# Row-wise infinity norm: the loads change queues after the 24th, GpSimd's setup waits for row 0, output copies are issued last

## The chip, the cores and the metric

One core of a Trainium2 chip runs the kernel. The metric is the device time of one execution in microseconds, as the median of several runs. Smaller is better.

## The reference

```
x: float32 [8192, 8192], normally distributed
out = np.linalg.norm(x, ord=np.inf, axis=1)      # out[i] = max over j of |x[i, j]|, float32 [8192]
```

The whole input, 268 MB, has to be read once. The output is 32 KB.

## The kernel before, in words

The 8192 rows are 64 groups of 128, one row of a group on each of the 128 partitions. The code calls such a group a "row" (R = 64). VectorE does all the arithmetic: `absmax` (line 62) is one tensor_reduce with the operation max and the absolute value, which takes a stretch of a row in SBUF to one number per partition. A dense reading of the loop (lines 90 to 138) goes like this.

- **Units.** The list PIECES (lines 18 to 24) has 36 units. Units 0 to 3 (HEAD) are single rows of 8192 elements. Units 4 to 26 are pairs: two rows of x that are neighbours in memory lie behind one another on the same partition, so one load brings 16384 elements (64 KB) per partition, 4096 KB for each row of the pair. Units 27 to 31 are pairs cut into two or three pieces, and units 32 to 35 are single rows cut into ever smaller pieces, the last of 896 elements.
- **The ring.** Loads land in `ring`, which holds three pairs (RING = 3 * 16384 elements per partition). Buffers are taken one after the other; `at` goes back to zero at the end. A load into a part of the ring waits for the data that landed there before, and for the VectorE instruction that read them. The very last piece has a tile of its own, `last`.
- **The loads.** Line 108 issues all 53 of them on SyncE (SP), in the order of the program.
- **The partial maxima.** Rows 0 to 47 go straight to `res` (63 columns, lines 118 to 121). Rows from CUT = 48 up, the four single rows of HEAD among them (rows 56 to 59), come in up to K = 4 pieces, each to a column of its own in `part` (line 130). The pieces of the very last row go into the last columns of `last` (line 128), so that its final reduction (line 110) takes them along.
- **Setup.** GpSimd clears `part` (line 52, since not every row has four pieces) and makes the identity matrix `ident` (line 54: a memset and an affine_select), which TensorE uses to transpose.
- **The output.** After the unit before the last, line 134 takes `part` to the last 15 columns of `res`. `pairs_out` (lines 77 to 86) transposes 56 columns on TensorE, ScalarE copies the result from PSUM and stores it by its own queue; `singles_out` (lines 67 to 75) does the same for 7 columns. The last row is transposed at line 142, copied by VectorE and stored by SP (lines 143 and 144).

The tile framework puts in the semaphore waits; each engine and each queue works through its instructions in order.

Of the kernel before, what the change touches and what calls it, by code (L numbers as in the profile page):

```python
# [1 line left out]

# [5 lines left out]

P = 128
FP32 = mybir.dt.float32  # L10
MAX = mybir.AluOpType.max

HEAD = 4
PAIRS = 28
PIECES = (
    [[8192]] * HEAD
    + [[16384]] * 23  # L20
    + [[8192, 8192], [7232, 9152], [6720, 9664], [8640, 7744], [5568, 5568, 5248]]
    + [[4480, 3712], [3392, 1920, 2880], [2752, 1600, 2048, 1792]]
    + [[1792, 1664, 1472, 1280, 1088, 896]]
)
RING = 3 * 16384


CUT = 48
K = 4


@with_exitstack
def kernel(
    ctx: ExitStack,
    tc: tile.TileContext,
    x: bass.AP,
    out: bass.AP,
):
    nc = tc.nc
    n_rows, n_cols = x.shape  # L40
    R = n_rows // P
    assert R == 64 and n_cols == 8192

    X_ONE = 2 * PAIRS

    single = ctx.enter_context(tc.tile_pool(name="single", bufs=1))
    psum_pool = ctx.enter_context(tc.tile_pool(name="psum", bufs=1, space=bass.MemoryType.PSUM))

    ring = single.tile([P, RING], FP32)
    res = single.tile([P, R - 1], FP32)  # L50
    part = single.tile([P, R - 1 - CUT, K], FP32)
    nc.gpsimd.memset(part, 0.0)  # L52
    ident = single.tile([P, P], FP32)
    make_identity(nc, ident)


    n_last = len(PIECES[-1]) - 1
    w_last = PIECES[-1][-1]
    last = single.tile([P, w_last + n_last], FP32)
    fin = single.tile([P, 1], FP32)  # L60

    def absmax(dst, src):
        nc.vector.tensor_reduce(  # L63
            out=dst, in_=src, axis=mybir.AxisListType.X, op=MAX, apply_absolute_value=True,
        )

    def singles_out():
        n = R - 1 - X_ONE
        ps = psum_pool.tile([n, P], FP32, name="ps_singles")
        sb = single.tile([n, P], FP32, name="sb_singles")  # L70
        nc.tensor.transpose(ps, res[:, X_ONE:], ident)  # L71
        nc.scalar.copy(sb, ps)  # L72
        nc.scalar.dma_start(
            out=out[X_ONE * P : (R - 1) * P].rearrange("(r p) -> r p", p=P), in_=sb
        )

    def pairs_out():
        sb = single.tile([PAIRS, P, 2], FP32, name="sb_pairs")
        both = res[:, :X_ONE].rearrange("p (g r) -> p g r", r=2)
        for r in range(2):  # L80
            ps = psum_pool.tile([PAIRS, P], FP32, name=f"ps_pairs{r}")
            nc.tensor.transpose(ps, both[:, :, r], ident)  # L82
            nc.scalar.copy(sb[:, :, r], ps)  # L83
        nc.scalar.dma_start(
            out=out[: X_ONE * P].rearrange("(g p r) -> g p r", p=P, r=2), in_=sb
        )

    at = 0
    next_pair, next_one = 0, X_ONE
    for u, widths in enumerate(PIECES):  # L90
        k = sum(widths) // n_cols
        if k == 2:
            row, next_pair = next_pair, next_pair + 2
        else:
            row, next_one = next_one, next_one + 1
        src = x[row * P : (row + k) * P].rearrange("(p r) m -> p (r m)", r=k)
        off = 0
        n_part = {}
        for h, w in enumerate(widths):
            final = u == len(PIECES) - 1 and h == n_last  # L100
            if final:
                buf = last[:, :w]
            else:
                if at + w > RING:
                    at = 0
                buf = ring[:, at : at + w]
                at += w
            nc.sync.dma_start(out=buf, in_=src[:, off : off + w])  # L108
            if final:
                absmax(fin[:, :1], last)  # L110
                break
            s = 0
            while s < w:
                r = row + (off + s) // n_cols
                left = n_cols - (off + s) % n_cols
                c = (w - s) // n_cols if left == n_cols else 0
                if c and r + c <= CUT:
                    absmax(
                        res[:, r : r + c],
                        buf[:, s : s + c * n_cols].rearrange("p (c m) -> p c m", m=n_cols),  # L120
                    )
                    s += c * n_cols
                    continue
                e = min(w, s + left)
                i = n_part.get(r, 0)
                n_part[r] = i + 1
                if r == R - 1:
                    absmax(last[:, w_last + i : w_last + i + 1], buf[:, s:e])
                else:
                    absmax(part[:, r - CUT, i : i + 1], buf[:, s:e])  # L130
                s = e
            off += w
        if u == len(PIECES) - 2:
            nc.vector.tensor_reduce(  # L134
                out=res[:, CUT:], in_=part, axis=mybir.AxisListType.X, op=MAX,
            )
            pairs_out()
            singles_out()

    fin_ps = psum_pool.tile([1, P], FP32)  # L140
    fin_sb = single.tile([1, P], FP32)
    nc.tensor.transpose(fin_ps, fin, ident)  # L142
    nc.vector.tensor_copy(out=fin_sb, in_=fin_ps)  # L143
    nc.sync.dma_start(out=out[(R - 1) * P :].rearrange("(r p) -> r p", p=P), in_=fin_sb)


# [1 line left out]
_INS = ['x']  # L148
_OUTS = [((8192,), 'float32')]


# [23 lines left out]
```

## Time and profile before

| what | us |
|---|---|
| median of 3 runs (630.62 to 630.86) | 630.73 |
| the profiled execution | 630.84 |
| its span, from the first to the last instruction | 629.1 |
| VectorE busy, 59 instructions | 552.6 (88% of the span) |
| one reduction of a pair, 16384 elements | 17.22 |
| one reduction of a row, 8192 elements | 8.69 |
| median from issue to landing of a pair's load | 40.8 |
| issue of the last load, line 108 | 614.48 |
| reduction of `part`, line 134 | 617.12 |
| last store issued, line 144 | 627.13 |

The DMA engines moved 268.49 MB at a mean of 427 GB/s over the span. All loads are on the queue q1 (SP's, 7634 packets), the two early stores on q10 (ScalarE's, 56 packets). ScalarE's other work is 2.0 us in all, GpSimd's 0.8 us and TensorE's 1.2 us.

How to read it: the views of waits give the engine, the instruction, what it waited for, then the total, the number of times and the longest. The timeline gives start, duration, engine, line and operation, and in brackets the idle time before it with what ended it. The table by stretches gives the stretch and its length, then the busy time of TensorE, its weight loads, VectorE, ScalarE and GpSimd, the clock of TensorE, the DMA engines' share and GB/s. DMA lines give the queue, its packets, MB and the share of 16 engines' time.

### The profile page before, as it was taken

Reading aid. Unit: us, or ns where it says so; the run is one execution under the profiler, and the core shown is the slowest. Engines: PE = TensorE matmul, PEld = TensorE weight load, DVE = VectorE, ACT = ScalarE, POOL = GpSimd, SP = SyncE. Lnnn points to the kernel's source line nnn. Section 1 sums busy time; section 2 is a strip of 40 time slices with the busy share of each in tenths; the row PEclk is TensorE's granted clock in tenths of the full one; section 3 lists DMA queues with packets and bytes.
Section 4 is the critical chain, followed back from the end, with each engine's and each line's share of the span. In section 5 each row is a group of like instructions: output and inputs, shape, how many; then the busy total and the mean of one; then the engine's idle time right before and its main releaser. Section 6 shows DMA issues by size and latency. Waiting matters only on the chain.

```text
span 629.1 us, 217 instructions
## 1 busy us (share of the span) xinstructions
PE 1.2 (0%) x4; PEld 0.3 (0%) x4; DVE 552.6 (88%) x59; ACT 2.0 (0%) x4; POOL 0.8 (0%) x7
## 2 busy tenths in 40 slices
PE   0000000000000000000000000000000000000000
PEld 0000000000000000000000000000000000000000
DVE  1983988889988889888898888998888999999998
ACT  0000000000000000000000000000000000000000
POOL 0000000000000000000000000000000000000000
DMA  8999999999999999999999999999999999999996
GB/s 367 433 467 404 463 404 463 400 467 404 463 404 463 404 463 404 463 404 463 404 463 404 463 408 458 408 458 408 458 408 429 431 447 432 427 426 424 425 423 265
DMA packets 7692, 268.49 MB, mean 427 GB/s; under 512 B 870, under 2 KB 906, under 8 KB 2058
## 3 DMA queue, kind: packets, MB, share of 16 engines
q1 hardware_dynamic: 7634, 268.44, 99.0%
q10 hardware_dynamic: 56, 0.03, 0.0%
q14 instruction: 2, 0.02, 0.0%
HBM read 268.44 MB, written 0.03 MB: 427 GB/s over the span
## 4 chain that ended last, share of the span: by engine, by line
DMA 57%; DVE 43%; issue 0%; SPq 0%; PE 0%
DMA ring<-in_x_dram 57%; DVE res L63 25%; DVE part L63 17%; DVE last L63 1%; DVE fin L63 0%; SPq L108 0%; PE fin_ps L142 0%; DVE fin_sb L143 0%; DVE res L134 0%
## 5 line engine op out<-in xcount | busy, mean ns | idle before, releaser
L63 DVE TENSOR_REDUCE res<-ring 128x2 f32<-128x16384 f32 (+1 forms) x25 | 413.2, 16536 | 57.6 <-DMA ring<-in_x_dram 57.6
L63 DVE TENSOR_REDUCE part<-ring 128x1 f32<-128x8192 f32 (+19 forms) x26 | 130.0, 5067 | 16.3 <-DMA ring<-in_x_dram 16.3
L63 DVE TENSOR_REDUCE last<-ring 128x1 f32<-128x1792 f32 (+4 forms) x5 | 8.0, 1662 | 0.0
L83 ACT COPY sb_pairs<-ps_pairs 28x128 f32<-28x128 f32 x2 | 0.5, 264 | 615.9 <-PE ps_pairs L82 615.9
L82 PE MATMUL ps_pairs<-ident,res 128*28 128x128 f32 x2 | 0.6, 394 | 617.5 <-DVE res L134 617.5
L83 ACT ACT_TABLE_LOAD x1 | 1.3, 1283 | 0.7 <-PEq L159 0.7
L63 DVE TENSOR_REDUCE fin<-last 128x1 f32<-128x901 f32 x1 | 1.1, 1091 | 0.0
L143 DVE COPY fin_sb<-fin_ps 1x128 f32<-1x128 f32 x1 | 0.3, 279 | 0.5 <-PE fin_ps L142 0.5
L82 PEld LDWEIGHTS ps_pairs<-ident,res 128*28 128x28 f32 x2 | 0.1, 106 | 617.5 <-issue 617.5
L71 PE MATMUL ps_singles<-ident,res 128*7 128x128 f32 x1 | 0.4, 417 | 0.0
L142 PE MATMUL fin_ps<-ident,fin 128*1 128x128 f32 x1 | 0.4, 373 | 8.1 <-DVE fin L63 8.1
masks.py:199 POOL TENSOR_SCALAR_AFFINE_SELECT ident<-ident 128x128 f32<-128x128 f32 x1 | 0.3, 292 | 0.1
L72 ACT COPY sb_singles<-ps_singles 7x128 f32<-7x128 f32 x1 | 0.3, 254 | 0.0
L134 DVE TENSOR_REDUCE res<-part 128x15 f32<-128x60 f32 x1 | 0.2, 216 | 0.0
masks.py:197 POOL MEMSET ident<- 128x128 f32 x1 | 0.2, 204 | 0.0
L52 POOL MEMSET part<- 128x60 f32 x1 | 0.1, 148 | 0.3 <-POOLq L159 0.3
L71 PEld LDWEIGHTS ps_singles<-ident,res 128*7 128x7 f32 x1 | 0.1, 132 | 0.1
L159 POOL MEMSET const-bfloat16-1.0<- 128x1 bf16 x1 | 0.1, 102 | 0.0
L159 POOL MEMSET const-uint8-127<- 128x1 uint8 x1 | 0.1, 102 | 0.0
L159 POOL MEMSET const-float32-0.0<- 128x1 f32 x1 | 0.1, 98 | 0.2 <-issue 0.2
L159 POOL MEMSET const-float32-1.0<- 128x1 f32 x1 | 0.1, 98 | 0.0
L142 PEld LDWEIGHTS fin_ps<-ident,fin 128*1 128x1 f32 x1 | 0.1, 80 | 8.6 <-DVE fin L63 8.6
## 6 DMA issues: line engine op xcount, KB each, us to landing
ring<-in_x_dram SPq DMA_DIRECT2D x6, 4096.0 KB, 21.7
ring<-in_x_dram SPq DMA_DIRECT2D x2, 2784.0 KB, 39.3
ring<-in_x_dram SPq DMA_DIRECT2D x1, 4832.0 KB, 40.7
ring<-in_x_dram SPq DMA_DIRECT2D x1, 4576.0 KB, 40.6
ring<-in_x_dram SPq DMA_DIRECT2D x1, 4320.0 KB, 34.1
ring<-in_x_dram SPq DMA_DIRECT2D x1, 3872.0 KB
ring<-in_x_dram SPq DMA_DIRECT2D x1, 3616.0 KB, 30.1
ring<-in_x_dram SPq DMA_DIRECT2D x1, 3360.0 KB
```

The costliest lines, as they stand in the source:

```text
L52: nc.gpsimd.memset(part, 0.0)
L63: nc.vector.tensor_reduce(out=dst, in_=src, axis=mybir.AxisListType.X, op=MAX, apply_absolute_value=True,)
L71: nc.tensor.transpose(ps, res[:, X_ONE:], ident)
L72: nc.scalar.copy(sb, ps)
L82: nc.tensor.transpose(ps, both[:, :, r], ident)
L83: nc.scalar.copy(sb[:, :, r], ps)
L134: nc.vector.tensor_reduce(out=res[:, CUT:], in_=part, axis=mybir.AxisListType.X, op=MAX,)
L142: nc.tensor.transpose(fin_ps, fin, ident)
L143: nc.vector.tensor_copy(out=fin_sb, in_=fin_ps)
L159: nc = _bacc.Bacc("TRN2", target_bir_lowering=False, num_devices=1)
```

## The change

Four things are different.

1. The first HEAD + SP_PAIRS = 24 units are loaded by SP as before, and all later ones by ScalarE's queue. The call `keep_in_program_order` keeps the issue order as written.
2. GpSimd's setup stands in a function `setup`, called once, after the first row's reduction. Both memsets get a manual dependency on that reduction. The memset of `part` leaves out column 0 of each row, which a reduction always writes; the identity's memset is written out, and the affine_select follows.
3. `pairs_out` and `singles_out` are called after the loop and not in it, so that their copies and stores come behind all loads on ScalarE.
4. `absmax` returns its instruction, for the dependency.

```diff
+SP_PAIRS = 20
...
-    nc.gpsimd.memset(part, 0.0)
     ident = single.tile([P, P], FP32)
-    make_identity(nc, ident)
...
+    def setup(after):
+
+        for ins in (nc.gpsimd.memset(part[:, :, 1:], 0.0), nc.gpsimd.memset(ident, 0.0)):
+            tc.add_manual_dep(
+                ins.ins, after.name,
+                mybir.DependencyInfo(mybir.DependencyClass.Sync, mybir.DependencyReason.DATA),
+                reason="not before the first row is in",
+            )
+        make_identity(nc, ident, nomemset=True)
...
-            nc.sync.dma_start(out=buf, in_=src[:, off : off + w])
+            queue = nc.sync if u < HEAD + SP_PAIRS else nc.scalar
+            tc.keep_in_program_order(
+                queue.dma_start(out=buf, in_=src[:, off : off + w])
+            )
...
-                    absmax(part[:, r - CUT, i : i + 1], buf[:, s:e])
+                    red = absmax(part[:, r - CUT, i : i + 1], buf[:, s:e])
+                    if u == 0:
+                        setup(red)
...
-            pairs_out()
-            singles_out()
 
+    pairs_out()
+    singles_out()
     fin_ps = psum_pool.tile([1, P], FP32)
```

## Prediction

> I count the units of the loop over PIECES by its u: 0 to 3 are the single rows of HEAD, 4 to 26 the pairs that come in one load, 27 to 31 the pairs in pieces, 32 to 35 the single rows of the tail. All times are microseconds unless marked.
>
> **What bounds the kernel now.** First the busy slices of the page:
>
> ```profile
> DVE  1983988889988889888898888998888999999998
> DMA  8999999999999999999999999999999999999996
> GB/s 367 433 467 404 463 404 463 400 467 404 463 404 463 404 463 404 463 404 463 404 463 404 463 408 458 408 458 408 458 408 429 431 447 432 427 426 424 425 423 265
> ```
>
> The DMA engines are full from end to end, VectorE nearly so. Who waits for whom, and then the same view from 400 on:
>
> ```profile
> DVE res L63 <- DMA ring<-in_x_dram: 57.6, 23, 10.7
> DVE part L63 <- DMA ring<-in_x_dram: 16.3, 4, 13.3
> ...
> DVE res L63 <- DMA ring<-in_x_dram: 12.8, 6, 2.1
> DVE fin_sb L143 <- PE fin_ps L142: 0.5, 1, 0.5
> ```
>
> VectorE waits for data only. After 400 it waits six times, 2.13 each. The timeline says where they are:
>
> ```profile
> 410.08 17.22 DVE L63 TENSOR_REDUCE res<-ring 128x2 f32<-128x16384 f32 x1 [2.13 <-DMA ring<-in_x_dram]
> 429.44 17.22 DVE L63 TENSOR_REDUCE res<-ring 128x2 f32<-128x16384 f32 x1 [2.14 <-DMA ring<-in_x_dram]
> 448.80 17.22 DVE L63 TENSOR_REDUCE res<-ring 128x2 f32<-128x16384 f32 x1 [2.14 <-DMA ring<-in_x_dram]
> 468.15 17.22 DVE L63 TENSOR_REDUCE res<-ring 128x2 f32<-128x16384 f32 x1 [2.13 <-DMA ring<-in_x_dram]
> 487.50 17.22 DVE L63 TENSOR_REDUCE res<-ring 128x2 f32<-128x16384 f32 x1 [2.13 <-DMA ring<-in_x_dram]
> ```
>
> Unit 4 starts at 61.71 and each later pair 19.36 after the one before, so these are units 22 to 26. A pair costs VectorE 17.22 and the loads 19.36. After 487.50 there is no gap any more. The stretches confirm it:
>
> ```profile
> 487.50:506.90 19.40, 0.00 (x0) 0.00 (x0) 19.40 (x2) 0.00 (x0) 0.00 (x0) 1.00 1.00 432
> 506.90:626.40 119.50, 0.80 (x3) 0.27 (x3) 119.39 (x31) 0.68 (x3) 0.00 (x0) 1.00 0.98 417
> ```
>
> The third busy figure is VectorE's: 19.40 of 19.40, then 119.39 of 119.50. So up to 487.50 the loads set the pace with VectorE 2.13 per pair to spare, and from there to 626.4 **VectorE alone is the path**. Lateness that VectorE still has at 487.50 goes to the end in full. Last, the chain that ended last, an excerpt:
>
> ```profile
> 446.67 0.02 issue
> 446.69 40.79 DMA ring<-in_x_dram
> 487.48 0.03 issue
> 487.50 34.40 DVE res L63 x3
> ```
>
> A load is issued when VectorE lets its buffer go and lands 40.8 later: it waits some 20 behind the load ahead of it, then moves for 19.4. Two loads are always in the queue.
>
> **What the Trainium skill says.** "DMA: Bandwidth & Descriptors", section "Queues, rings and completion order": each DMA engine goes round robin between the queue rows that have work, packet by packet (roughly 9 to 17 descriptors each); within one ring descriptors are taken in order. The same page, "Issuing engines are not separate DMA queues": SP's and ScalarE's transfers share the same 16 engines, so two issuers save issue time alone. The trace before shows two queues together only at the end: the 28 KB store of L84 is issued on ScalarE's queue at 618.40, with loads still waiting on SP's. The DMA view of 619.02 to 621.97, and then of 621.90 to 622.50:
>
> ```profile
> q1 hardware_dynamic: 277, 1.18, 99.1%
> ...
> q1 hardware_dynamic: 65, 0.20, 84.1%
> q10 hardware_dynamic: 42, 0.03, 15.1%
> ```
>
> For about 3.0 only SP's q1 moves (1.18 MB, 74 KB per engine, 17 packets), then both mix, and loads queued earlier still follow. So queues do mix, behind what the engines have already taken; whether that is a number of bytes (one packet of a pair load) or of packets (all of one) isn't shown. "SBUF — State Buffer", "Who interferes with whom": a tensor_reduce never contends with GpSimd on trn2; no row before shows them together. "ScalarE: Activation LUTs", "What ACT_TABLE_LOAD costs": 1283 ns, and the trace has 1283.
>
> **The change part by part.**
>
> *Loads move to ScalarE from unit 24 on.* HEAD + SP_PAIRS = 24, so SP keeps units 0 to 23; the 29 loads of 24 to 35 go to ScalarE, with the same two waits each (old data landed, VectorE done with it). Issue costs nothing: 0.33 per load on SP, once in 19.36, and ScalarE is idle before 617.9. What changes is the **hand-over**. Unit 24's load goes out when VectorE is through with unit 21: 390.73 + 17.22 = about 408.0, as before. At that time unit 22 has its last 2.1 to landing (410.08), and unit 23, issued at 388.6 on SP's queue, hasn't begun. In one queue 23 goes wholly before 24. In two they take turns. A pair load is 8.39 MB in packets of 65.5 KB (the DMA view of 388 to 410: 9.44 MB in 176 packets, 32 of them tiny), thus 8 per engine, each 19.36 / 8 = 2.42. I take it that one packet of 23 is ahead of 24's first (the bytes reading of the store: 74 KB is about one) and then 7 alternate with 7: unit 23 lands 7 x 2.42 = 16.9 late, at 446.4 in place of 429.44. Unit 24 lands at 448.8, as it would have.
>
> *What VectorE makes of it.* It starts unit 23 16.9 late. The gaps ahead of 24, 25 and 26 absorb 2.14 + 2.13 + 2.13 = 6.4, for their data are there in time. At unit 26 it is 16.9 - 6.4 = **10.5 late**, and all after that is VectorE without a gap.
>
> *Does the DMA run dry?* Unit 26 needs 23's buffer: free at 446.4 + 17.2 = 463.6, while unit 25 keeps the DMA busy until 468.2. The margin is 4.6; what a 4 MB load needs beyond its transfer is about 13.2 - 0.7 - 9.7 = 2.8 (issue of the first at 0.74, start of its row at 13.30, one row 9.7). Later margins grow by 2.1 each. Cost zero; without that cover at most 2.8 of DMA idleness, itself under VectorE's lag.
>
> *Setup behind the first row.* Three GpSimd steps (0.15 + 0.20 + 0.29 = 0.64) move from 0.73 to about 22.0, the end of row 0. Nothing is queued behind them on GpSimd. If the next row's reduction had to wait for the memset of part, it would have 22.93 - 21.99 = 0.95 of idle to do so, and later units 2.1 each. The first need of part's other columns is unit 28's, after 520; of ident, PE's at 617. Cost zero; 0.6 if the cover were gone. Gain at the front: SP issues at 0.74 behind the common start, not behind GpSimd, so zero, 0.3 at best.
>
> *Copies and early stores behind the loads.* PE waits for L134 as before. Copies (0.26 x 2 + 0.25) and stores (0.62 + 0.28) come after ScalarE's last load, which went out at 614.48 before and is bounded by the same buffers and landings. The table load (1.28), should it slip behind the loads, is done before L134. From L134 to the fin store there are 627.13 - 617.12 = 10.0, and the chain needs 0.6 + 0.8 + 0.9 + 3.5 (the stores' last bytes, by 622.9, less the issue's end at 619.4) + 1.3 = 7.1. Cost zero; if the order slipped by over 3 it would show one for one. The fin store is on SP in both, with nothing ahead.
>
> **Sum.** 0 + 10.5 + 0 + 0. The profiled execution is 630.84 (span 629.1, 1.74 around it), 0.11 over the median 630.73. Span to 639.6, profiled 641.3, **median 641.2**, 1.7% slower.
>
> **The rivals.** The unknown is n, how many of unit 23's 8 packets are ahead of 24's first on the worst engine. The delay at the end is (8 - n) x 2.42 - 6.4.
>
> *No sharing in effect (not slower).* The engines take in by packets, some 17 as in the store's wait, so that all 8 of unit 23 are ahead; or ScalarE's first load starts late. Then nothing moves: 630.7. It decides from n = 6 (4.8 under the 6.4 of slack). For it: 17 packets fit the store's wait as well as 74 KB; against it: those were packets of 4 to 6 KB, and taking in 16 of 65.5 KB would mean over 1 MB per engine. Chance 0.14.
>
> *ScalarE's packet goes first (n = 0).* The turn passes after unit 22's last packet, which ends just when 24 arrives (issue at 408.0 plus about one). One engine is enough, since a load has landed when all 16 have. 19.4 - 6.4 = 13.0: 643.7. Whole loads in turns with 24 first give the same. For it: the near tie; against: the store's wait. Chance 0.22.
>
> *Two to five packets ahead.* 8.1, 5.7, 3.3 and 0.9: 638.8 to 631.6; n = 2 is likeliest. Chance 0.14, of it 0.12 for 2 and 3.
>
> *Strict preference for ScalarE.* Loads 24 and 25 (issued at 427.3) both pass 23, which lands at 468.2 with an empty queue behind it: 38.8 - 6.4 = 32.4, 663. Against it: the mixing at 622. With other slow outcomes 0.04.
>
> *Faster.* Only the front could give, 0.3, which is too little to be seen; 0.02 for what I don't see.
>
> **How the numbers follow.** n = 1 has 0.44 and gives the 641.2. Range 636.0 to 645.0: n = 0 to 3, 0.44 + 0.22 + 0.12, and a part of the slow rest, about 0.8; left out are no sharing, n = 4 and 5, the gain, and over 645. About 0.2% is what a measurement of this kernel can tell from no change. Slower 0.83, same 0.15 (no sharing, and n = 5 with 0.01), faster 0.02.
>
> **What would show it.** Unit 23's reduction starts at 444 to 449 after a wait of 17 to 19, the only long one after 62; units 24 on then start without a gap, unit 26 at 498; VectorE is unbroken from 446 to 637; DMA bytes end near 624 as before, some 12 ahead of VectorE, in place of 2. q10 carries the loads of the second half. Wrong if unit 23 starts at 429.4 (no sharing), if a second gap opens after it (the ring ran dry), or if VectorE's start of row 1 leaves 22.9 (setup).

## The result, and the profile after

The changed kernel takes 648.36 us (648.16 to 648.55, 6 runs) against 630.67 (630.47 to 630.86, 6 runs): ratio 1.0281, 95% interval 1.0267 to 1.0294. That is 17.7 more, 7.2 over the forecast and 3.4 over the top of its range. The direction was right, and so was the place; the size was not. Times are microseconds unless marked.

The span went from 629.1 to 646.4. VectorE's busy time is the same, 552.5, so the difference is waiting. The busy slices of the kernel after:

```profile
DVE  1893898888898888898888898842999799999998
DMA  9999999999999999998998999999818999999996
GB/s 383 428 442 434 454 426 418 454 430 414 454 442 402 454 450 393 454 454 389 454 454 389 454 454 397 446 454 422 357 65 389 422 428 440 435 416 436 423 419 282
```

Two holes are new. VectorE has one in the 27th and 28th slice (about 420 to 452), where the DMA engines are full. The DMA engines have one in the 29th and 30th (452 to 485), with 65 GB/s in the second of them, where VectorE is full. The prediction had the first and said that there would be no second. The waits of the kernel after:

```profile
DVE res L63 <- DMA ring<-in_x_dram: 75.3, 21, 21.6
DVE part L63 <- DMA ring<-in_x_dram: 16.1, 4, 13.0
```

The pairs' wait rose from 57.6 to 75.3, 17.7, and its longest from 10.7 to 21.6. The timeline around the hand-over:

```profile
409.83 17.22 DVE L63 TENSOR_REDUCE res<-ring 128x2 f32<-128x16384 f32 x1 [2.13 <-DMA ring<-in_x_dram]
448.70 51.47 DVE L63 TENSOR_REDUCE res<-ring 128x2 f32<-128x16384 f32 x3 [21.65 <-DMA ring<-in_x_dram]
504.81 34.41 DVE L63 TENSOR_REDUCE res<-ring 128x2 f32<-128x16384 f32 x3 [4.63 <-DMA ring<-in_x_dram]
```

Before, the reductions stood at 410.08, 429.44, 448.80 and so on. Now unit 22 is followed by 21.65 of waiting, then three reductions without a gap, then 4.63 of waiting that the prediction doesn't have, and the rest without a gap. Unit 26 starts at 504.81 in place of 487.50: 17.3 late, which is the whole difference of the spans. Two stretches of the table by time after, from unit 25's landing to shortly after the load of unit 26 goes out, and from unit 26's reduction to the end of VectorE's work on rows:

```profile
467.80:484.10 16.30, 0.00 (x0) 0.00 (x0) 16.30 (x2) 0.00 (x0) 0.00 (x0) 1.00 0.07 24
...
504.81:643.70 138.89, 0.80 (x3) 0.27 (x3) 138.79 (x32) 1.97 (x4) 0.00 (x0) 1.00 0.98 419
```

The DMA share of the first is 0.07: the engines stand still for about 16. And the second says, as before, that what is late at unit 26 goes to the end in full.

Why they stand still is read from the queue. The timeline of ScalarE's queue:

```profile
483.08 17.95 ACTq L120 DMA_DIRECT2D ring<-in_x_dram  x5
```

The first of these five is the load of unit 26. It needs the buffer of unit 23. Had VectorE begun with unit 23 at 448.70, the buffer would have been free at 465.9; it became free at 483.05, with the second of the three reductions. The trace shows the order: the 24th reduction (unit 23's place, as units count from 0) waits for the semaphore that unit 24's load raises, and the 25th for that of unit 23. **The two reductions changed places.** The change pins the loads by `keep_in_program_order`, not the reductions. With one queue and no pin they stay in order (traces of e2 and e3 below).

### The profile page after: what moved, and what is told of

It reads as the page before. It is cut to its first block, busy times and chain, and to the rows that moved or that the text cites. A ratio compares the mean times of both kernels' runs of the same rounds, so it can differ in the third digit from the quotient of the medians.

```text
span 646.4 us, 218 instructions
## 1 busy us (share of the span) xinstructions
PE 1.2 (0%) x4; PEld 0.3 (0%) x4; DVE 552.5 (85%) x59; ACT 2.0 (0%) x4; POOL 0.8 (0%) x7
## 4 chain that ended last, share of the span: by engine, by line
DMA 55%; DVE 44%; issue 1%; SPq 0%; PE 0%
DMA ring<-in_x_dram 55%; DVE res L63 27%; DVE part L63 16%; DVE last L63 1%; SPq L120 0%; DVE fin L63 0%; PE fin_ps L157 0%; DVE fin_sb L158 0%; DVE res L149 0%
## 5 line engine op out<-in xcount | busy, mean ns | idle before, releaser
L63 DVE TENSOR_REDUCE res<-ring 128x2 f32<-128x16384 f32 (+1 forms) x25 | 413.1, 16536 | 75.3 <-DMA ring<-in_x_dram 75.3
```

The lines of the kernel that those rows point to most:

```text
L63: return nc.vector.tensor_reduce(out=dst, in_=src, axis=mybir.AxisListType.X, op=MAX, apply_absolute_value=True,).ins
```

## The experiments

Each expectation stands as it was written before the run. Theory A: the order of the two reductions is what makes the ring run dry, and this sets the time. Theory B: sharing the DMA engines alone (two queues have loads under way at once) sets it, and the order is a side effect.

**e1_order_kept**: both queues and the hand-over stay, VectorE's order is pinned.

```diff
-        return nc.vector.tensor_reduce(
+        return tc.keep_in_program_order(nc.vector.tensor_reduce(
             out=dst, in_=src, axis=mybir.AxisListType.X, op=MAX, apply_absolute_value=True,
-        ).ins
+        )).ins
```

> The changed kernel with VectorE's reductions pinned to the order of the program, so that unit 23 comes before unit 24; two queues and the hand-over stay. Theory A (the order was swapped, so unit 23's buffer came free one reduction late and the ring ran dry): unit 23 starts near 448.5, its buffer is free near 466, unit 26's load goes out then and the DMA has no hole; the lag is 19.3 less three gaps of 2.13, 12.9, so 643.5. Theory B (sharing the engines alone sets the time, the order is a side effect): 648, with the hole of 16 us in the DMA still there.

Measured: 643.35 (643.08 to 643.42), ratio 1.0200, interval 1.0186 to 1.0214. Its timeline from unit 22 on, and the same stretch of time as above:

```profile
409.94 17.22 DVE L63 TENSOR_REDUCE res<-ring 128x2 f32<-128x16384 f32 x1 [2.14 <-DMA ring<-in_x_dram]
448.65 77.19 DVE L63 TENSOR_REDUCE res<-ring 128x2 f32<-128x16384 f32 x5 [21.49 <-DMA ring<-in_x_dram]
```

```profile
467.80:484.10 16.30, 0.00 (x0) 0.00 (x0) 16.30 (x2) 0.00 (x0) 0.00 (x0) 1.00 0.89 386
```

The long wait of VectorE is the same (21.49), so sharing is as it was. The hole in the DMA is gone but for a small rest (0.89 in place of 0.07), and with it the wait of 4.63 ahead of unit 26. Sharing alone costs 12.7, close to the 12.9 of A; the swap on top of it costs 5.0 (648.36 less 643.35).

**e4_swap_alone**: SP issues every load, so nothing is shared; VectorE's order is pinned as in e1, but with unit 24 ahead of unit 23 (an excerpt; the lines of e1's edit are left out).

```diff
-SP_PAIRS = 20
+SP_PAIRS = 60
...
+SWAP = 23
...
-                    absmax(
+                    todo = (
...
+                    if u == SWAP:
+                        held = todo
+                    else:
+                        absmax(*todo)
+                    if u == SWAP + 1:
+                        absmax(*held)
```

> SP issues all loads, nothing is shared, but VectorE is made to reduce unit 24 before unit 23. Theory A: VectorE starts unit 24 at 448.8, unit 23 ends near 483.2, unit 26's load is issued there with the queue empty from about 468 on, lands near 505: 648.3, as the changed kernel without any sharing. Theory B: 630.7 to 637, since the data are there in time.

Measured: 648.20 (648.09 to 648.24), ratio 1.0278, interval 1.0264 to 1.0292. Its timeline:

```profile
409.86 17.22 DVE L64 TENSOR_REDUCE res<-ring 128x2 f32<-128x16384 f32 x1 [2.14 <-DMA ring<-in_x_dram]
448.55 51.47 DVE L64 TENSOR_REDUCE res<-ring 128x2 f32<-128x16384 f32 x3 [21.47 <-DMA ring<-in_x_dram]
504.65 17.22 DVE L64 TENSOR_REDUCE res<-ring 128x2 f32<-128x16384 f32 x1 [4.63 <-DMA ring<-in_x_dram]
```

Line for line the picture of the changed kernel, with one queue. In the same place VectorE waits 21.47, here because it insists on unit 24 while unit 23 lies ready. The swap alone is enough for the whole loss; with the swap there, sharing adds nothing, since unit 23 isn't wanted before 465.8. Theory B falls.

**e2_one_queue_sp** (SP_PAIRS = 60; the late setup, copies and stores stay) and **e3_one_queue_act** (`queue = nc.scalar` for all loads).

> SP issues all loads; the late setup and the late copies and stores of the change stay. Theory A and B (the hand-over is the whole cost): 630.7, as before. Rival (setup or late stores cost some of it): over 631.5.

> ScalarE's queue issues all loads from the first, so there is no hand-over. Theory A and B: 630.7, since the queue itself costs nothing. Rival C (ScalarE's queue is the slower issuer): some tenths per load, 632 to 640.

Measured: 630.69 (ratio 1.0000, interval 0.9992 to 1.0008) and 630.74 (1.0002, 0.9994 to 1.0011), against 630.63. The setup behind row 0 and the late outputs cost nothing that can be seen, and ScalarE's queue is as good an issuer as SP's. All of the loss is in the hand-over and the order that came with it. The four versions with everything else of the change in them, side by side:

| | reductions in order | 24 ahead of 23 |
|---|---|---|
| one queue | 630.69 (e2) | 648.20 (e4) |
| two queues, late hand-over | 643.35 (e1) | 648.36 (the change) |

e1 and e4 have the reductions pinned, the other two don't; that the pin itself costs nothing to speak of is seen in e8 below (631.01 with it). In e2 the setup falls into the wait that was there before anyway:

```profile
21.93 0.14 POOL L69 MEMSET part<- 128x45 f32 x1 [21.49 <-DVE part L63]
22.00 0.20 POOL L69 MEMSET ident<- 128x128 f32 x1
22.28 0.29 POOL masks.py:199 TENSOR_SCALAR_AFFINE_SELECT ident<-ident 128x128 f32<-128x128 f32 x1
22.90 8.69 DVE L63 TENSOR_REDUCE part<-ring 128x1 f32<-128x8192 f32 x1 [1.03 <-DMA ring<-in_x_dram]
```

The next pair separates two kinds of lateness by moving the hand-over to the front. VectorE's own lag should be absorbed by 17 pairs of slack; time in which the DMA engines stand still should not. **e5_early_kept** has the order pinned as in e1, **e6_early_free** has it as the framework puts it; both have SP_PAIRS = 6.

> As e1_order_kept (two queues, VectorE's order pinned), but SP hands over after 6 pairs in place of 20. Theory A: unit 9 starts some 19.3 late; 17 pairs follow with 2.13 of slack each, 36 in all, so the lag is gone long before the tail: 630.7. Theory B (sharing costs time for good, since two queues move less): about 643, as with the late hand-over.

> As the changed kernel with 6 pairs on SP in place of 20, VectorE's order not pinned; the compiled order has unit 10 before unit 9. Theory A: the lag of VectorE would be absorbed, but the DMA stands still for some 16 and the loads set the pace from there to the tail, so the 17.3 stay: 648. Theory B' (all that is late early is absorbed): 630.7.

Measured: e5 632.94 (631.60 to 633.88, ratio 1.0033, interval 1.0023 to 1.0043), e6 648.83 (1.0286, 1.0271 to 1.0302), against 630.65. In e6 the hole is at 197 to 213, and nothing of it comes back:

```profile
197.00:213.00 16.00, 0.00 (x0) 0.00 (x0) 16.00 (x2) 0.00 (x0) 0.00 (x0) 1.00 0.00 0
```

e5 comes back almost: 2.3 stay, where 0 was expected, and its executions lie further apart than those of the kernel before (631.60 to 633.88). The timeline of e5, then that of the kernel before, for units 17 and 18:

```profile
315.57 17.22 DVE L63 TENSOR_REDUCE res<-ring 128x2 f32<-128x16384 f32 x1 [0.78 <-DMA ring<-in_x_dram]
334.98 17.22 DVE L63 TENSOR_REDUCE res<-ring 128x2 f32<-128x16384 f32 x1 [2.19 <-DMA ring<-in_x_dram]
```

```profile
313.31 17.22 DVE L63 TENSOR_REDUCE res<-ring 128x2 f32<-128x16384 f32 x1 [2.13 <-DMA ring<-in_x_dram]
332.65 17.22 DVE L63 TENSOR_REDUCE res<-ring 128x2 f32<-128x16384 f32 x1 [2.13 <-DMA ring<-in_x_dram]
```

VectorE has caught up and waits again, but the loads themselves are 2.3 late. The packets and semaphore events of the trace show where: the load of unit 12 went out at 194.93, when the queue held only the end of unit 11 (landed at 197.0). On two of the 16 engines its first packet began at 197.8 and 197.9, on the others at 196.1 to 196.9. From then on the 16 landings of a load lie 2.0 to 2.2 apart from first to last, to the end of the kernel, where they were 0.5 apart; a load has landed when the last engine is through. But a load issued this late isn't always hurt: in e1 the load of unit 26 went out at 465.90 with unit 25 landing at 467.98, the same 2.1, and its landings lay 0.6 apart, about 0.5 late in all. The guess that the late issue is behind e5's 2.3 made a prediction of its own, **e8_early_halves_kept**: as e5, with the two units that share cut in halves, so that the buffer comes free earlier.

```diff
-    + [[16384]] * 23
+    + [[16384]] * 5 + [[8192, 8192]] * 2 + [[16384]] * 16
```

> As e5_early_kept, but units 9 and 10, the two that share, come in two loads of 8192 each. Theory A2 (the 2.3 that e5_early_kept lost come from the load of unit 12, issued only 2 before the queue was empty, so that two engines began it late and stayed behind): in halves unit 9's buffer is free some 9 earlier, no engine runs empty, and the lag is absorbed: 630.7, with the engines' landings still within 0.8 of each other at the end. Rival (each hand-over costs about 2 of DMA time by itself): 633.

Measured: 631.01 (630.73 to 631.23), ratio 1.0004, interval 0.9996 to 1.0013. The landings stay about 0.7 apart up to 572 (from 578 on 1.1, over the 0.8 expected), and the lag is gone by 255.15, where the kernel before has 255.25:

```profile
176.53 77.25 DVE L63 TENSOR_REDUCE res<-ring 128x1 f32<-128x8192 f32 x6 [10.74 <-DMA ring<-in_x_dram]
255.15 17.22 DVE L63 TENSOR_REDUCE res<-ring 128x2 f32<-128x16384 f32 x1 [1.37 <-DMA ring<-in_x_dram]
```

So a hand-over by itself needn't cost anything that can be seen, and the rival of about 2 for each hand-over falls. The load of unit 12 goes out at 185.25 here, 12 ahead of unit 11's landing at 197.07. That supports the guess and doesn't show it: the halves change the size of the packets too, and why two engines were late in e5 and none in e1 stays open.

**e7_halves_kept**: as e1, late hand-over, units 23 and 24 in halves.

```diff
-    + [[16384]] * 23
+    + [[16384]] * 19 + [[8192, 8192]] * 2 + [[16384]] * 2
```

> As e1_order_kept, but units 23 and 24, the two that share, come in two loads of 8192 each. Theory A (the delay is the time in which the other queue's packets of equal number pass): the first half of unit 23 lands near 429, the second near 448.5; VectorE ends unit 23 near 457 and not 466, 8.6 late at unit 24, less two gaps of 2.13: 635.0. Theory C (the delay belongs to the change of queue, whatever the size): about 643.

Measured: 634.02 (633.70 to 634.16), ratio 1.0052, interval 1.0037 to 1.0067. Of the 12.7 of e1, 3.4 are left.

```profile
427.87 8.69 DVE L63 TENSOR_REDUCE res<-ring 128x1 f32<-128x8192 f32 x1 [0.99 <-DMA ring<-in_x_dram]
447.29 77.31 DVE L63 TENSOR_REDUCE res<-ring 128x1 f32<-128x8192 f32 x7 [10.73 <-DMA ring<-in_x_dram]
```

VectorE starts the halves of unit 23 at 427.87 and 447.29; the second is 1.36 ahead of unit 23's start in e1, of which 0.28 is this execution running ahead of e1's already at unit 22. The 1.1 left is about the 1.0 by which the time is better than expected; I had not allowed for the smaller packet (last section).

## Why the prediction was wrong, step by step

- *What bounds the kernel*: right. VectorE's gaps of 2.13 and its unbroken work from unit 26 on decide what its lag is worth: three gaps lie behind the late hand-over (e1), 17 behind the early one (e5, e8). One reading was off, without effect on the sum: the view from 400 on counts the wait of 388.6 to 390.7 ahead of unit 21 with it, so five gaps lie after 400 and not six.
- *Issue on ScalarE's queue, setup, copies and stores at zero*: right, together within about 0.1% (e2, e3).
- *The hand-over shares the engines*: right, packet by packet, with one or two of unit 23's packets ahead. The DMA view of the kernel after, 409.8 to 443.0 and then 445.7 to 447.9:

```profile
q10 hardware_dynamic: 112, 7.34, 51.1%
q1 hardware_dynamic: 108, 7.08, 49.2%
...
q10 hardware_dynamic: 24, 0.79, 82.9%
q1 hardware_dynamic: 10, 0.00, 0.3%
```

The two queues take turns on the engines, and get half of them each. That they take turns packet by packet is what the Trainium skill says ("DMA: Bandwidth & Descriptors", "Queues, rings and completion order"). But here they alternate after each 64 KB piece: if such a piece is one descriptor, which no run shows, a packet of 9 to 17 descriptors, as given there, would have let the 8 pieces and the closing one of unit 23 through together.

- *"unit 23 lands 7 x 2.42 = 16.9 late, at 446.4"*: 2.4 too little. Its data were in by 445.6. Yet the small packets that signal the landing also wait for their turn: 14 of the 16 come at 447.5 to 448.1 (ten of them are the q1 packets of the second window above), behind one more packet of unit 24. In e1 VectorE starts unit 23 at 448.65, and one queue would have had it start at 409.94 + 19.36 = 429.30, which is 19.35 earlier. So 19.35 - 6.4 = 12.95, against 12.7 measured in e1: the mechanism was right, the term a packet short. The rival with ScalarE's packet first has about e1's time, 643.7, but by luck: it wanted no packet of unit 23 ahead, and one or two were.
- *"Does the DMA run dry? ... Cost zero"*: **the step that failed.** It took for granted that VectorE works through the units in the order of the code, so that unit 23's buffer, which unit 26 needs, would be free at 463.6. In the changed kernel that buffer is free at 483.05, one reduction of 17.2 later. The load of unit 26 goes out at 483.08 and takes 21.7 to VectorE: 504.81. Against 487.50 that is the 17.3. e1 takes the swap away and gets 643.35, inside the range; e4 has the swap without the sharing and gets 648.20. Of the 7.2 that the forecast was short, the swap makes 5.0 and the missing packet 2.2 (643.35 less 641.2).
- *"The margin is 4.6"* was off too: with unit 23's landing at 448.5 it was about 2, and 2 is not always enough (e5). In e1 unit 26 lands at 487.88, which is under VectorE's lag (it gets there at 500.04) and costs nothing.
- *What would show it*: the sign of a reduction starting at 444 to 449 came true by luck, at 448.70, but it is unit 24's, and the wait is 21.65 and not 17 to 19. The sign of being wrong, "a second gap opens after it", came true too: the 4.63.
- The rivals had the ring running dry only under a strict preference for ScalarE's queue (663). A change of VectorE's order wasn't among them, and the range ended at 645.

Still open is why the framework puts unit 24 first. The effect is seen in the traces of the kernel after and of e6, both with two queues and no pin; its rule for ordering was not tried out.

## What to carry to other kernels

When a stream of loads changes its queue, read the consumer's compiled order, not only that of the loads: pinning the producers doesn't pin the consumer, and in a ring a swap of two consumers keeps the older buffer for a whole step longer. Price a delay by who is late: here the consumer's lag was paid back out of its slack (e5, e8), while time in which the resource that sets the pace stood still was not (e6). If a hand-over must be, put it where slack follows, pin both sides, and cut the loads that overlap (631.01 in place of 648.36); none of the versions here beats the kernel before.

## What the runs showed of the hardware that I had not expected

- The signal of a landing queues like data. After unit 23's last data packet (445.6) 14 of its 16 semaphore packets came at 447.5 to 448.1, behind a packet of the other queue of 2.42; with 32 KB packets (e7) the second landing is some 1.1 earlier, close to the 1.2 that such a packet is shorter.
- DMA engines kept their distance. In e5 two of 16 engines began one load about 1.5 after most of the others, and the landings stayed about 2.1 apart for the next 400, worth 2.3 at the end. The engines were full in that time (a share of 1.01 from 252 to 300), which left them no slack in which to catch up.
